# A hybrid backbone on one core: the first six filler steps of each layer take two PSUM banks in turn

## The chip, the cores and the metric

The kernel runs on one core of one Trainium2 chip. The metric is the device time of one execution in microseconds (us), as the median of several runs. Times inside an execution come from one profiled execution of the kernel before. PE is the matrix engine (TensorE), DVE the vector engine, ACT the scalar engine, POOL the GpSimd engine, SP the engine that issues most DMAs.

## The reference

Two layers of a diffusion backbone work on 1024 latent tokens of width 1024 and, in the first layer, on 256 context tokens too. Cut to what matters here:

```
def hybrid_layer(x, xc, ...):
    u  = modulate(rmsnorm(x,  n1), sh1, sc1)   @ w_in
    uc = modulate(rmsnorm(xc, n1), csh1, csc1) @ w_in
...
    ym, ymc = mlstm_mixer(...)      # 4 heads
    yn, ync = na_mixer(...)         # 8 heads, neighbourhood attention
    yl, ylc = lru_mixer(...)
    x = x + g1[:, None] * (jnp.concatenate([ym, yn, yl], axis=-1) @ w_out)
    x = x + g2[:, None] * sq_relu_mlp(modulate(rmsnorm(x, n2), sh2, sc2), w1, w2)
    if want_ctx:
        xc = xc + cg1[:, None] * (jnp.concatenate([ymc, ync, ylc], axis=-1) @ w_out)
        xc = xc + cg2[:, None] * sq_relu_mlp(modulate(rmsnorm(xc, n2), csh2, csc2), w1, w2)
```

The change concerns the product with `w_out`, and of it the part that needs only `ym` and `yl`: this half can be computed while the attention that makes `yn` is still running.

## The kernel before, in words

Activations lie feature by token. The token axis has blocks of 256 (context) and twice 512 (latent) columns, `BLKS`. A float32 product is made of three matmuls on split operands (a rounded high part and a low remainder): high times high, low times high, high times low. `load_w` loads a piece of weight (DMA, L197), ACT makes the high part (L200) and DVE the low part (L201). `split` does the same for activations (L210, L211).

PSUM has eight banks of 512 columns: one named p, one q, three a, two b, one c. `bank("pq")` takes the letters in turn, `bank("p")` always the same. Tiles of one bank are taken in the order of the program: a tile can be written when the one before it in the bank has been read.

Each layer has an attention stage, of four pairs of heads. `na_att` runs units of K x Q products (L825, L829, banks a), a softmax on DVE (L839, L843) and ACT (L846), transposes of the weights of attention (L718, `softmax_pv`, banks b, b, q in turn) and their product with V (L748, bank c). Between the units `side()` is called, 40 times in the first layer and 32 times in the second. It puts in a piece of `na_prep` for the next pair of heads and the steps of the filler that are due.

`na_prep` loads a piece of q or k (`ut`, DMA L672, two buffers), scales it on DVE (L675), transposes it on PE (L683, L685, bank b for the first pair of heads, then b, b, q in turn), splits it (L691, L692 for K, L696, L697 for Q), and copies parts to the other half of the partitions by DMA (L699, L702, L703). Positional bias tables (`tab`, L799) and V blocks (`VB`, L808) are loaded too.

The filler is `fill()`, which runs `oproj` on half 0 of the output projection. A step is twelve matmuls (L1354) into one tile of 256 or 512 columns, and then `ev_half`: a DMA load of the residual `xs` (L1370, three buffers, so the fourth load waits until the first store has gone), the eviction on DVE (L1371, scaled and added to `xs`), and the store (L1372). In the first layer the steps alternate between 256 and 512 columns for sixteen steps, and eight of 512 follow; in the second there are sixteen of 512. In the listings the first six steps of the first layer have the tiles 5946, 6107, 6208, 6365, 6520, 6599, those of the second 21757, 21936, 22100, 22248, 22436, 22615.

The order on each engine is not the order of the program. A scheduler places each instruction by its own estimates and keeps what data, buffers and banks demand. Each engine, and the queue of SP with its DMAs, then works its list strictly from the front: an instruction that waits holds all that stand behind it.

Of the kernel before, what the change touches and what calls it, by code (L numbers as in the profile page):

```python
# [91 lines left out]
def backbone_kernel(ctx: ExitStack, tc: tile.TileContext, I, out, dbg=None):  # L92
# [13 lines left out]
    def nm(s):  # L106
        seq[0] += 1
        return f"{s}_{seq[0]}"
# [17 lines left out]
    def bank(tag):  # L126

        if len(tag) > 1:
            turn[tag] = turn.get(tag, -1) + 1
            tag = tag[turn[tag] % len(tag)]  # L130
        return ps.tile([P, 512], F32, name=nm("ps" + tag), tag="ps" + tag, bufs=PSB[tag])
# [54 lines left out]
    def load_w(src, shape, early=False):  # L186


        raw = wp.tile([P, WSZ], F32, name=nm("wr"), tag="wr", bufs=2)
        hi = wp.tile([P, WSZ], F32R, name=nm("wh"), tag="wh", bufs=2)  # L190
        lo = wp.tile([P, WSZ], F32R, name=nm("wl"), tag="wl", bufs=2)
        n = shape[0] * shape[1]
        raw3 = raw[:, :n].rearrange("p (k c) -> p k c", k=shape[0])
        srcs = src if isinstance(src, list) else [src]
        m = shape[0] // len(srcs)
        for i, s_ in enumerate(srcs):
            sp.dma_start(raw3[:, i * m:(i + 1) * m], s_)  # L197
        cuts = [0, n // 4, n // 2, n] if early else [0, n]
        for a, b in zip(cuts, cuts[1:]):
            act.activation(hi[:, a:b], raw[:, a:b], AF.Copy)  # L200
            dve.tensor_sub(lo[:, a:b], raw[:, a:b], hi[:, a:b].bitcast(F32))  # L201
        return (hi[:, :n].rearrange("p (k c) -> p k c", k=shape[0]),
                lo[:, :n].rearrange("p (k c) -> p k c", k=shape[0]))
# [5 lines left out]
    def split(hi, lo, src32):  # L209
        act.activation(hi, src32, AF.Copy)  # L210
        dve.tensor_sub(lo, src32, hi.bitcast(F32))  # L211
# [236 lines left out]
    def wbank():  # L448
        wseq[0] += 1
        return bank("pqaaa")  # L450
# [155 lines left out]
    for l in range(DEPTH):  # L606
# [264 lines left out]
        with tc.tile_pool(name=f"m1_{l}", bufs=1, reuse_waits="tile") as m1:  # L871
            phase(f"lru_in{l}")

            with tc.tile_pool(name=f"lru_{l}", bufs=1, reuse_waits="tile") as lp, \
# [76 lines left out]
                for ct in range(2):  # L951
# [9 lines left out]
                    for d in range(2):  # L961
                        c4 = d * 2 + ct
                        gates = []
                        for gi in range(2):
# [3 lines left out]
                            for (o, n) in ((0, 512), (512, 512), (1024, 259)):  # L968
                                t = bank("a")
# [357 lines left out]
        def y_load(dst, blks, half, tp):  # L1327

            for i, (kt, r) in enumerate(YROWS[half]):
                if r == 7:  # L1330
                    continue
                for bi in blks:
# [2 lines left out]
                    sp.dma_start(yl_[:, :n], yT_d[l][r * P:(r + 1) * P, off:off + n])  # L1335
                    split(dst[bi][0][:, i], dst[bi][1][:, i], yl_[:, :n])

        def oproj(Y, blks, half, wide, evac, pre=None):

            for c2 in range(4):  # L1340
                cs = slice(c2 * 256, c2 * 256 + 256)
                rows = ((0, 2), (6, 8)) if half == 0 else ((2, 6),)
                w = load_w([I["w_out"][l, a * P:b * P, cs].rearrange("(k p) c -> p k c", p=P) for a, b in rows], (4, 256))
                if pre:
                    pre(blks, c2)
                for cc in range(2):
                    ct = c2 * 2 + cc
                    for bi in blks:
                        n = BLKS[bi][1]
                        t = wbank() if wide else bank("p")  # L1350
                        i = 0
                        for k in range(4):
                            for (a, b) in ((0, 0), (0, 1), (1, 0)):
                                pe.matmul(t[:, :n], w[a][:, k, cc * P:(cc + 1) * P], Y[bi][b][:, k],  # L1354
                                          start=(i == 0), stop=(i == 11))
                                i += 1
                        evac(t[:, :n], bi, ct)
                        yield
# [3 lines left out]
        with tc.tile_pool(name=f"na_{l}", bufs=1, reuse_waits="tile") as npl, \  # L1362
# [11 lines left out]
            def fill():  # L1374

                for part in parts:
                    phase(f"oproj{l}")
                    Yh = {bi: [yp.tile([P, 4, BLKS[bi][1]], F32R, name=nm("yh"), tag=f"yh{min(bi, 1)}{j}")
                               for j in range(2)] for bi in part}
                    y_load(Yh, part, 0, yp)  # L1380
                    for _ in oproj(Yh, part, 0, False, ev_half):
                        yield
                        phase(f"oproj{l}")
# [55 lines left out]
        with tc.tile_pool(name=f"mlp_{l}", bufs=1, reuse_waits="tile") as rp:  # L1439
# [12 lines left out]
            def oproj_end(blks, between=None):  # L1452
                def ev(t, bi, ct):
                    v = 1 if BLKS[bi][2] else 0
                    dve.scalar_tensor_tensor(xr[bi][:, ct], t, G1[:, ct, v:v + 1], xr[bi][:, ct],
                                             op0=OP.mult, op1=OP.add)
                    stat_add(acc2, bi, xr[bi][:, ct], ct, yk)

                for i, _ in enumerate(oproj(Y, blks, 1, True, ev, x_rows)):
                    if between and i == 2 * len(blks) - 1:  # L1460
                        between()
# [141 lines left out]
```

## Time and profile before

| what | us |
|---|---|
| median of 3 runs | 3117.27 |
| lowest and highest of the runs | 3112.53, 3120.43 |
| the profiled execution | 3115.3 |
| its span on the core | 3113.5 |
| PE busy in the span | 3013.0 |
| DVE busy | 1903.4 |
| ACT busy | 1130.1 |
| attention stage of layer 0, about | 505 to 745 |
| attention stage of layer 1, about | 2125 to 2345 |

The profiled execution lies 2.0 us below the median of the runs and 1.8 us above its own span. Busy time says how long an engine had an instruction running; a busy PE can run at either of two clock levels, and PEclk gives the mean granted clock as a share of the upper one.

### The profile page before, as it was taken

The numbers are of one execution on the slowest core, as the hardware profiler recorded it, in microseconds if no ns is written. First come the engines' busy times: TensorE is split into PE (matmuls) and PEld (weight loads), VectorE is DVE, ScalarE is ACT, GpSimd is POOL, SyncE is SP. The second block draws the span as 40 slices with busy tenths as digits, with TensorE's granted clock in tenths as the row PEclk, the third lists the DMA queues.
The fourth block names the chain that finished last, engine by engine and source line by source line (L and its number), as shares of the span: only waits on it lengthen the run. The fifth ranks groups of instructions, "written<-read, shape, count | busy, mean of one in ns | idle before, by whom it ended". The sixth has DMA issues, their size and how long they took to land.

```text
span 3113.5 us, 47480 instructions
## 1 busy us (share of the span) xinstructions
PE 3013.0 (97%) x18250; PEld 2550.8 (82%) x18250; DVE 1903.4 (61%) x4334; ACT 1130.1 (36%) x2027; POOL 283.9 (9%) x252
## 2 busy tenths in 40 slices
PE   7999998999999999999999999998899999999999
PEld 6888898877888888887778889997787777787777
DVE  6757654786977666555444484866788444444444
ACT  5632223565422222233233353234574222332222
POOL 0410010121200000010000411002222000000000
PEclk9999999999999999999999999999999999999999
DMA  8624567765233444233323542348763333333233
GB/s 273 216 73 134 175 187 204 217 179 185 68 109 109 122 129 122 78 112 95 95 88 96 161 143 81 98 129 231 220 179 99 95 95 93 97 115 93 90 96 93
DMA packets 506138, 410.72 MB, mean 132 GB/s; under 512 B 27197, under 2 KB 471577, under 8 KB 505913
## 3 DMA queue, kind: packets, MB, share of 16 engines
q1 hardware_dynamic: 494488, 387.41, 41.7%
q0 software_dynamic: 8576, 15.00, 1.5%
q10 hardware_dynamic: 2848, 5.28, 0.5%
q8 instruction: 144, 2.36, 0.3%
q14 instruction: 82, 0.66, 0.1%
HBM read 339.72 MB, written 67.53 MB: 131 GB/s over the span
## 4 chain that ended last, share of the span: by engine, by line
PE 71%; DVE 10%; DMA 9%; issue 2%; ACT 2%; SPq 1%; ACTq 0%; DVEq 0%
PE psa L461 15%; PE psa L1526 14%; PE psq L461 5%; PE psp L461 5%; PE psp L1526 5%; PE psq L1526 5%; PE psp L476 4%; PE psq L476 4%; DMA mr<-in_w_mod_dram 4%; PE psp L1354 2%; DVE ma L337 2%; PE psc L748 2%; PE psa L1354 1%; PE psb L718 1%; DVE wl L201 1%
## 5 line engine op out<-in xcount | busy, mean ns | idle before, releaser
L200 ACT ACTIVATE wh<-wr 128x1024 fp32r<-128x1024 f32 (+3 forms) x372 | 363.3, 985 | 927.1 <-PE psa L1526 311.3
L201 DVE TENSOR_TENSOR wl<-wr,wh 128x1024 fp32r<-128x1024 f32 (+3 forms) x372 | 426.8, 1152 | 386.2 <-ACT wh L200 379.7
L461 PE MATMUL psa<-xh,wh 128*128 128x512 f32 (+1 forms) x856 | 319.7, 374 | 2.4 <-ACT xh L436 2.2
L461 PE MATMUL psa<-xh,wl 128*128 128x512 f32 (+1 forms) x856 | 319.5, 374 | 1.4 <-DVE wl L201 1.4
L461 PE MATMUL psa<-xlo,wh 128*128 128x512 f32 (+1 forms) x856 | 320.0, 374 | 0.4 <-DVE xlo L437 0.4
L1526 PE MATMUL psa<-hl,wh 128*128 128x512 f32 (+1 forms) x768 | 286.2, 373 | 0.8 <-DVE hl L211 0.8
L1526 PE MATMUL psa<-hh,wh 128*128 128x512 f32 (+1 forms) x768 | 284.7, 376 | 0.3 <-ACT wh L200 0.3
L1526 PE MATMUL psa<-hh,wl 128*128 128x512 f32 (+1 forms) x768 | 278.1, 373 | 0.6 <-DVE wl L201 0.6
L1530 DVE SCALAR_TENSOR_TENSOR res<-psa,modt,res 128x512 f32<-128x512 f32 (+1 forms) x192 | 131.0, 693 | 170.1 <-PE psa L1526 169.9
L461 PEld LDWEIGHTS psa<-xh,wh 128*128 128x128 f32 x856 | 161.3, 188 | 34.1 <-ACT xh L436 2.4
L461 PEld LDWEIGHTS psa<-xh,wl 128*128 128x128 f32 x856 | 161.3, 189 | 33.0 <-DVE wl L201 2.2
L461 PEld LDWEIGHTS psa<-xlo,wh 128*128 128x128 f32 x856 | 161.5, 189 | 31.7 <-DVE xlo L437 0.6
L210 ACT ACTIVATE hh<-rl 128x512 fp32r<-128x512 f32 (+1 forms) x160 | 93.8, 589 | 220.4 <-DVE rl L1492 220.3
L1526 PEld LDWEIGHTS psa<-hh,wh 128*128 128x128 f32 x768 | 144.4, 188 | 34.7 <-ACT wh L200 8.7
L402 POOL TENSOR_TENSOR acc<-acc,nsq 128x512 f32<-128x512 f32 (+1 forms) x56 | 77.0, 1380 | 1024.5 <-ACT nsq L401 1023.8
L1526 PEld LDWEIGHTS psa<-hh,wl 128*128 128x128 f32 x768 | 144.5, 188 | 28.7 <-DVE wl L201 1.5
L1526 PEld LDWEIGHTS psa<-hl,wh 128*128 128x128 f32 x768 | 144.5, 188 | 27.6 <-DVE hl L211 1.1
L476 PE MATMUL psp<-wl,xh 128*128 128x256 f32 (+1 forms) x560 | 161.7, 289 | 5.4 <-DVE wl L201 5.2
L476 PE MATMUL psp<-wh,xh 128*128 128x256 f32 (+1 forms) x560 | 161.4, 288 | 3.3 <-ACT wh L200 3.3
L476 PE MATMUL psq<-wh,xh 128*128 128x256 f32 (+1 forms) x560 | 162.0, 289 | 1.2 <-ACT usq L632 0.7
L476 PE MATMUL psq<-wl,xh 128*128 128x256 f32 (+1 forms) x560 | 160.2, 286 | 0.0
L476 PE MATMUL psq<-wh,xlo 128*128 128x256 f32 (+1 forms) x560 | 159.9, 286 | 0.0
(409 smaller groups left out, 7326.1 us busy)
## 6 DMA issues: line engine op xcount, KB each, us to landing
wr<-in_w_mlp_dram SPq DMA_DIRECT2D x256, 512.0 KB
wr<-in_w_in_dram SPq DMA_DIRECT2D x48, 512.0 KB
mr<-in_w_mod_dram SPq DMA_DIRECT2D x48, 512.0 KB
mr<-in_w_mod_dram SPq DMA_DIRECT2D x22, 1024.0 KB
tab<-T_d SPq DMA_DIRECT2D x48, 384.0 KB
T_d<-E_d POOLq DMA_DIRECT2D x48, 256.0 KB, 6.6
ab<-row_d SPq DMA_DIRECT2D x36, 256.0 KB
xT_d<-res SPq DMA_DIRECT2D x4, 2048.0 KB
```

The lines of the kernel that those rows point to most:

```text
L200: act.activation(hi[:, a:b], raw[:, a:b], AF.Copy)
L201: dve.tensor_sub(lo[:, a:b], raw[:, a:b], hi[:, a:b].bitcast(F32))
L210: act.activation(hi, src32, AF.Copy)
L337: dve.scalar_tensor_tensor(a, raw[:, k], s[:, k], a, op0=OP.mult, op1=OP.add)
L402: pool.tensor_add(acc[bi], acc[bi], sq[:, :n])
L461: m = pe.matmul(t[:, :n], w[a][:, k, :], X[bi][b][:, k, :], start=(i == 0), stop=(i == 23))
L476: m = pe.matmul(t[:, :cols], X[bi][b][:, half * 4 + k, o:o + P], ws[half][a][:, k, :], start=(i == 0), stop=(i == 23))
L718: pe.transpose(t[:w, j * P:(j + 1) * P], S[e][:, o:o + w], permT)
L748: pe.matmul(to[64 * e:64 * e + 64, :P], vals[i][:w, 64 * e:64 * e + 64], PT[:w, e, i], start=(i == 0), stop=(i == nt - 1))
L1354: pe.matmul(t[:, :n], w[a][:, k, cc * P:(cc + 1) * P], Y[bi][b][:, k], start=(i == 0), stop=(i == 11))
L1526: m = pe.matmul(t[:, :n], w[a][:, k, cc * P:(cc + 1) * P], H[bi, k][b], start=(i == 0), stop=(i == 3 * GH - 1))
L1530: dve.scalar_tensor_tensor(xr[bi][:, ct], t[:, :n], G2[:, ct, v:v + 1], xr[bi][:, ct], op0=OP.mult, op1=OP.add)
```

## The change

A counter is put in for each layer, and the first six tiles that `oproj` takes outside the wide case come from `bank("pq")`. These are the first six filler steps of the layer: p, q, p, q, p, q. From the seventh on the bank is p, as before. Lines behind the edit move by four, so that the matmuls are L1358 and the eviction L1375.

```
+        n_half = [0]
+
         def oproj(Y, blks, half, wide, evac, pre=None):
...
                         n = BLKS[bi][1]
-                        t = wbank() if wide else bank("p")
+
+                        t = wbank() if wide else bank("pq" if n_half[0] < 6 else "p")
+                        n_half[0] += 1
                         i = 0
```

The number of instructions stays; their order in the two attention stages is new, and elsewhere it is as before. Three places show it.

DVE in layer 0, the difference of the two orders where the first `xs` load of those behind the K copies is used (L843 and L839 are attention's softmax):

```order
 L843 ISA S_6010,m_869_6012<-psa_5992,zcol,m_868_6011 128x256
 L843 ISA m_869_6012 128x1
-L1371 SCALAR_TENSOR_TENSOR xs_6378<-psp_6365,modt_119,xs_6378 128x512
+L1375 SCALAR_TENSOR_TENSOR xs_6533<-psp_6520,modt_119,xs_6533 128x256
 L839 ISA S_6088,m_886_6089<-psa_6074,tab_5984 128x384
 L839 ISA m_886_6089 128x1
```

The eviction of the fourth step (6365, 512 columns) is gone from here, and that of the fifth (6520, 256 columns) stands in its place; the second and fourth steps stand later, and the first, third and fifth have all gone by this point.

DVE in layer 1, at the first evictions, before (L692 and L697 make the low parts of K and Q, L675 scales a load):

```order
L1371 SCALAR_TENSOR_TENSOR xs_21770<-psp_21757,modt_120,xs_21770 128x512
L692 TENSOR_TENSOR KL_21515<-psb_21541,KH_21513 64x512
L697 SCALAR_TENSOR_TENSOR ql_21562<-psb_21557,gq_17233,QS_21511 64x512
L1371 SCALAR_TENSOR_TENSOR xs_21949<-psp_21936,modt_120,xs_21949 128x512
L697 SCALAR_TENSOR_TENSOR ql_21577<-psb_21572,gq_17233,QS_21510 64x512
L675 TENSOR_TENSOR ut_21648<-ut_21648,rsn_20574 128x256
L697 SCALAR_TENSOR_TENSOR ql_21577<-psb_21572,gq_17233,QS_21511 64x512
L675 TENSOR_TENSOR ut_21720<-ut_21720,rsn_20574 128x512
L1371 SCALAR_TENSOR_TENSOR xs_22113<-psp_22100,modt_120,xs_22113 128x512
```

The same place after:

```order
L1375 SCALAR_TENSOR_TENSOR xs_21770<-psp_21757,modt_120,xs_21770 128x512
L692 TENSOR_TENSOR KL_21515<-psb_21541,KH_21513 64x512
L697 SCALAR_TENSOR_TENSOR ql_21562<-psb_21557,gq_17233,QS_21511 64x512
L1375 SCALAR_TENSOR_TENSOR xs_22113<-psp_22100,modt_120,xs_22113 128x512
L697 SCALAR_TENSOR_TENSOR ql_21577<-psb_21572,gq_17233,QS_21510 64x512
L675 TENSOR_TENSOR ut_21648<-ut_21648,rsn_20574 128x256
L697 SCALAR_TENSOR_TENSOR ql_21577<-psb_21572,gq_17233,QS_21511 64x512
L675 TENSOR_TENSOR ut_21720<-ut_21720,rsn_20574 128x512
```

Before, the first three steps (21757, 21936, 22100) are evicted here; after, the first and the third are, and the second stands 81 rows behind the third.

SP in layer 1, with the K and Q copies of the pair of heads that follows (L699, L703) and the loads `ut_22345` and `ut_22417` of `na_prep`, before:

```order
L703 DMA KL_21647<-KL_21647 64x1280
L699 DMA QS_21643<-ql_21929 64x512
L672 DMA ut_22345<-u_nk_81 128x2x128
L1372 DMA xT_d<-xs_22628 128x512
L1370 DMA xs_22940<-xT_d 128x512
L197 DMA wr_23469<-in_w_out_dram 128x2x256 x2
L1370 DMA xs_23146<-xT_d 128x512
L197 DMA wr_23777<-in_w_out_dram 128x2x256 x2
L799 DMA tab_22304<-T_d_97 128x2x384
L672 DMA ut_22417<-u_nk_81 128x4x128
```

The same place after:

```order
L703 DMA KL_21647<-KL_21647 64x1280
L808 DMA VB_22157<-u_nv_83 32x4x128 x2
L672 DMA ut_22345<-u_nk_81 128x2x128
L699 DMA QS_21642<-ql_21929 64x512
L699 DMA QS_21643<-ql_21929 64x512
L672 DMA ut_22417<-u_nk_81 128x4x128
L699 DMA QS_21642<-ql_22024 64x512
L699 DMA QS_21643<-ql_22024 64x512
```

Before, four issues of `w_out` pieces (`wr`), two loads of `xs`, a store and a table stand between the two `ut` loads; after, the two stand close together, and the `w_out` pieces and `xs` loads come later.

## Rows read from the trace of the kernel before

**Rows 1.** The page: busy time by engine, and the chain's shares by engine

```profile
PE 3013.0 (97%) x18250; PEld 2550.8 (82%) x18250; DVE 1903.4 (61%) x4334; ACT 1130.1 (36%) x2027; POOL 283.9 (9%) x252
...
PE 71%; DVE 10%; DMA 9%; issue 2%; ACT 2%; SPq 1%; ACTq 0%; DVEq 0%
```

**Rows 2.** Line L1354: matmuls on p (ns), and idle before them, us, times

```profile
L1354 PE MATMUL psp<-yh,wh x320: 274/394/796, 514.8 to 2320.7; 128*128 128x512 f32 x128, 128*128 128x256 f32 x32
...
L1354 PE MATMUL psp<-yh,wl x160: 274/394/628, 516.0 to 2321.0; 128*128 128x512 f32 x128, 128*128 128x256 f32 x32
...
  DVE xs L1371: 17.5, 12
```

**Rows 3.** Stages: length, busy PE, PEld, DVE, ACT, POOL; PEclk, DMA share, GB/s

```profile
523.40:536.00 12.60, 8.98 (x65) 7.17 (x63) 8.68 (x18) 4.65 (x13) 6.96 (x4) 0.99 0.85 231
536.00:544.00 8.00, 5.35 (x23) 4.24 (x22) 3.49 (x15) 3.13 (x9) 0.00 (x0) 0.59 0.88 223
544.00:600.00 56.00, 55.33 (x452) 46.92 (x451) 44.78 (x137) 33.99 (x84) 11.02 (x6) 1.00 0.67 200
600.00:680.00 80.00, 71.43 (x591) 58.36 (x590) 68.98 (x216) 52.62 (x134) 14.53 (x8) 0.98 0.78 209
...
2150.00:2185.00 35.00, 33.76 (x262) 28.05 (x264) 29.82 (x88) 24.22 (x54) 5.07 (x2) 1.00 0.94 268
2185.00:2199.00 14.00, 9.68 (x43) 7.23 (x38) 12.31 (x31) 4.17 (x13) 3.61 (x2) 0.63 0.72 207
2199.00:2260.00 61.00, 56.99 (x463) 47.12 (x463) 47.97 (x143) 36.53 (x90) 14.62 (x8) 1.00 0.73 214
```

**Rows 4.** The chain in order of time, layer 0: start, duration, what

```profile
519.10 4.41 PE psp L1354 x12
...
569.04 1.43 PE psp L1354 x12
...
602.67 8.13 DMA KL<-KL
...
716.76 2.78 PE psp L1354 x12
```

**Rows 5.** SP in order of time, layer 0: start, duration, what, times

```profile
539.77 1.41 SPq L1370 DMA_DIRECT2D xs<-xT_d  x3
```

**Rows 6.** DVE in order of time, layer 0, with idle before and releaser

```profile
542.59 0.75 DVE L1371 SCALAR_TENSOR_TENSOR xs<-psp,modt,xs 128x512 f32<-128x512 f32 x1 [4.09 <-DMA xs<-xT_d]
```

**Rows 7.** PE in order of time, layer 1

```profile
2175.76 0.37 PE L829 MATMUL psa<-KH,QS 128*128 128x256 f32 x1
...
2188.38 0.69 PE L825 MATMUL psa<-KH,QS 128*128 128x384 f32 x1 [2.44 <-DVE m L839]
...
2191.42 0.58 PE L829 MATMUL psa<-KH,QS 128*128 128x256 f32 x1 [1.40 <-DVE m L843]
```

**Rows 8.** DVE in order of time, layer 1

```profile
2170.43 0.75 DVE L1371 SCALAR_TENSOR_TENSOR xs<-psp,modt,xs 128x512 f32<-128x512 f32 x1
...
2171.99 1.22 DVE L201 TENSOR_TENSOR wl<-wr,wh 128x1024 fp32r<-128x1024 f32 x1
...
2176.97 0.43 DVE L675 TENSOR_TENSOR ut<-ut,rsn 128x256 f32<-128x256 f32 x1 [2.16 <-DMA ut<-u_nk]
...
2186.14 1.68 DVE L675 TENSOR_TENSOR ut<-ut,rsn 128x512 f32<-128x512 f32 x1 [3.63 <-DMA ut<-u_nk]
```

**Rows 9.** Waits of PE, layer 1: us in total, times, longest

```profile
PE psa L825 <- DVE m L839: 5.0, 3, 2.4
```

**Rows 10.** SP in order of time, layer 1

```profile
2178.02 0.89 SPq L197 DMA_DIRECT2D wr<-in_w_out_dram  x2
...
2179.50 0.46 SPq L672 DMA_DIRECT2D ut<-u_nk  x1
```

**Rows 11.** The MLP of layer 0, columns as in rows 3

```profile
1100.00:1150.00 50.00, 50.00 (x287) 43.40 (x287) 34.13 (x82) 13.83 (x22) 0.00 (x0) 1.00 0.43 125
```

**Rows 12.** One group of PE in these 50 us: busy, mean ns | idle before

```profile
L461 PE MATMUL psp<-xh,wh 128*128 128x256 f32 (+1 forms) x16 | 5.4, 336 | 0.0
```

## The prediction

> **What bounds the kernel now.** I read the page first: TensorE is busy for 3013.0 us of a span of 3113.5, and the chain that ended last lies on PE for 71% and on DVE for 10% [rows 1]. So a change can win only idle PE time or time at the lower clock, about 100 us in all, and can lose by adding to either. Next I read the line that the change touches: L1354 has 320 + 160 matmuls on bank p, and before them PE stood idle 17.5 us, in 12 places, until an eviction (L1371) had emptied the bank [rows 2]. That is the wait which the second bank can remove. It is 0.6% of the span, and not all of it can be had, since only six steps of each layer are touched.
>
> Third, the busy time by stage over the two stretches where these steps stand [rows 3]. In layer 0, PE works 8.98 of 12.60 us up to 536, 5.35 of 8.00 at a mean granted clock of 0.59 up to 544, then 55.33 of 56, and again only 71.43 of 80 up to 680. In layer 1 it works 33.76 of 35 us up to 2185, then 9.68 of 14 at 0.63, then 56.99 of 61. The idle stretches are those in which attention waits for data, and the filler steps are what PE does meanwhile. Whether a step runs inside such a hole or after it decides what it costs.
>
> The price of a step is read from the chain in order of time [rows 4]: twelve matmuls of 512 columns take 2.78 us at the upper level (2.4 GHz), twelve of 256 columns 1.43, and the step at 519.10, after PE had idled, took 4.41, mostly at the lower level (1.2 GHz).
>
> **The change, layer 0.** No instruction is added; every second of six tiles goes to bank q. But q is also the bank of the next heads' transposes and of every third softmax tile, tiles of one bank are taken in program order, and the order is written anew. What comes out shows in the order of DVE. The landmark there is the eviction that uses the first xs load that SP issues behind the K copies, three at 539.77 [rows 5]: DVE stood 4.09 us for it, until 542.59, with attention's softmax queued behind it [rows 6]. That load keeps its place behind the same copies. In the old order it serves the fourth step's eviction, so PE has by then done four steps (256, 512, 256, 512 columns); in the new one it serves the fifth's, and the second and fourth, on q, come later: three steps of 256. The old order owed PE nothing at that point; the new one owes 2 x 2.8 less the 256-step done early, 1.4: 4.2 us of matmuls. They come in 544 to 600, where only 0.67 us is idle, so they sit on the path.
>
> Against this, DVE has one 0.75 us eviction fewer ahead of the landmark and the loads of one preparation are issued a little earlier: I take the landmark as 1.0 us earlier, bounds 0 and 4.1 (DVE's whole wait for it; below zero is excluded, since nothing is put ahead of the copies). With fewer matmuls to do while attention waits, new idle of 0.5 us, bounds 0 and 3. Sum: 4.2 - 1.0 + 0.5 = **+3.7 us**. The best end also regains the 0.7 idle and the 2.2 us that PE loses to the lower level in 536 to 544 (5.35 x 0.41): 4.2 - 4.1 - 0.7 - 2.2 = -2.8. The worst end is three steps in the open, 3 x 2.8 = +8.4.
>
> **The change, layer 1.** All steps have 512 columns. In the order, the second step's eviction has left its place and the third step's stands there instead; the second, fourth and sixth steps wait for bank q, and the steps behind them wait with them, because the three xs buffers go round: the fifth step's is the second's. By the K x Q product at 2175.76 [rows 7] the old order has done seven steps, the new one two: five steps, 5 x 2.8 = 14.0 us, are owed. In exchange DVE passes this stretch without three evictions of 0.75 and three weight splits of 1.22 [rows 8], 5.9 us together, and attention gets that far earlier; since DVE was not full there (29.82 of 35, [rows 3]) I take 4 of the 5.9, bounds 0 and 5.9.
>
> Then comes the hole. Before, PE waited 2.44 and 1.40 us for the softmax [rows 7], because DVE stood 2.16 and 3.63 us until preparation loads (ut) had landed [rows 8]; over the layer's stage the K x Q products wait 5.0 us for it, in three places [rows 9]. SP issues the second one at 2179.50, behind w_out loads [rows 10], and it lands at 2186.14 [rows 8], 6.6 us later. In the new order both ut loads stand ahead of those w_out loads. So part of the hole closes, and what is left of it is filled with owed steps. From 2175.8 to 2260 are 84.2 us. They hold 4.3 idle (2185 to 2199), 4.0 idle (2199 to 2260), and 4.2 lost to the clock: 0.63 over 14 us means 10.4 us at the lower level, some 8.4 of it busy, and half of that is loss. Work: 84.2 - 8.3 - 4.2 = 71.7, plus 14.0 owed is 85.7 us. Residual idle I take as 3 us (between 0, all holes filled, and 12.5, all of idle and clock loss still there). The stretch then ends at 2175.8 - 4 + 85.7 + 3 = 2260.5, **+0.5 us**; bounds 2175.8 - 5.9 + 85.7 = 2255.6 (-4.4) and 2175.8 + 85.7 + 12.5 = 2274.0 (+14.0).
>
> **Sum.** +3.7 + 0.5 = +4.2 us, bounds -7.2 and +22.4. Against the profiled execution, 3115.3 us, that is 3119.5. The median of the runs, 3117.3, lies 2.0 above it, and the same sum there gives 3121.5; I take 3120, between the two. The other edits of the diff (a counter and a choice of bank) cost the chip nothing.
>
> **Rivals.** *A, holes close fully.* The ut loads come early enough for DVE never to wait, so layer 1 goes to its best end, -4.4, and in layer 0 the owed 4.2 us fall into the 8.6 idle us of 600 to 680, where the chain goes through transfers (a K copy of 8.13 us, [rows 4]) and not through PE; with the landmark 4.1 earlier and the clock's 2.2 regained that is -6.3. Together -10.7: 3117.3 - 10.7 = 3106.6. For it: the early ut loads. Against it: 544 to 600 is full and lies before that hole, and PE then moves everything behind it.
>
> *B, the cover is gone.* Slower: the filler is what kept PE at work while attention waited for transfers. If attention stays bound by its loads and DVE (the DMA share is 0.94 in 2150 to 2185, [rows 3]), PE idles where the five steps stood, the clock falls sooner, and the steps come when PE is full. Layer 1 then costs its upper end, +14.0, layer 0 its 3.7: +17.7, 3135. The place is 2139 to 2176; it decides from about 8 us of residual idle instead of 3. For it: in the new order PE has no other work there. Against it: DVE's 5.9 us.
>
> *C, the clock falls because banks alternate.* Layer 0's MLP ran 50.00 of 50 us at a granted clock of 1.00 [rows 11] while it wrote p, q and a in turn (by `wbank`; its share on p is in [rows 12]), so alternation alone does not lower it here. Were it so, nine 512-steps would cost 4.41 - 2.78 = 1.63 more each and three 256-steps half that, together 17.1: 3137. The Trainium skill, "TensorE: Matmul & The Clock Gate", section "A second HAM failure mode: psum-queue depth-cycling", tells of a kernel that cycled through PSUM banks and idled so often between groups that its clock swung between the two levels. By that rule this would be the outcome; the stage at 1.00 does not bear it out.
>
> *D, nothing that counts.* The steps change places inside the same stage, and gains and debts cancel within 2 us: 3117.
>
> **Chances.** Forecast and D together 0.66 (0.45 and 0.21), A 0.14, B 0.17, C 0.03. About 0.3%, 9.4 us, is what a measurement of this kernel can tell from no change: below 3107.9 counts as faster, above 3126.6 as slower. Faster is A, 0.14; slower is B and C, 0.20; within is 0.66. The range from 3107 to 3132 takes in the bounds of the sum but for its far upper part, where B and C lie (some 0.12 is above it, 0.06 below).
>
> **What would show it.** Right: PE's idle until the L1371 eviction (L1375 in the new file) falls well under 17.5 us; three 256-steps precede the xs landmark; 536 to 544 has less PE work, 544 to 600 stays full; in layer 1 the waits of 2.16 and 3.63 on ut are gone or short and the stretch 2185 to 2199 has no stall of 2.44. Wrong: PE idle beyond 3 us between 2176 and 2260, or over 8 us more in 2139 to 2176 without attention coming earlier (B); a mean clock under 0.9 in 544 to 600 (C); or both stages ending early (A).

## The result: slower by 0.7%

The changed kernel takes 3139.7 us against 3120.0 for the kernel before (medians of six runs each): +19.7 us, a ratio of 1.0072 with an interval of 1.0056 to 1.0087. The forecast was 3120 with a range up to 3132. The profiled execution took 3139.4 us, its span is 3137.6, 24.1 above the span before; the profiled execution of the kernel before lies 4.7 us below its median, so the two profiles differ by 4.4 us more than the medians do.

The first rows are from the page of the kernel after: busy time by engine, and the shares of the chain that ended last.

```profile
PE 3022.3 (96%) x18250; PEld 2561.4 (82%) x18250; DVE 1901.3 (61%) x4334; ACT 1132.4 (36%) x2027; POOL 283.0 (9%) x252
...
PE 72%; DVE 10%; DMA 9%; issue 2%; ACT 2%; SPq 1%; ACTq 0%; DVEq 0%
```

The same 18250 matmuls keep PE busy 9.3 us longer than in [rows 1], at a mean granted clock of 0.985 in place of 0.991, so some ran at the lower clock level that had not; the rest of the 24.1 us is idle time. The view of the line of the output projection, with the idle time before it that the evictions ended:

```profile
L1358 PE MATMUL psp<-yh,wh x272: 274/394/628, 517.0 to 2346.1; 128*128 128x512 f32 x104, 128*128 128x256 f32 x32
...
L1358 PE MATMUL psq<-yh,wh x48: 390/394/502, 554.8 to 2242.6; 128*128 128x512 f32 x48
...
  DVE xs L1375: 16.2, 16
```

Six steps (48 matmuls with the high weights) went to q, the first of them at 554.8, where the second step of the kernel before began at 519.1 [rows 4]. And the wait for evictions hardly fell: 16.2 us where it was 17.5 [rows 2]. Both figures add up the idle time of PE and that of its weight loads (PEld), which run side by side. The views of PE's own waits give, before, in layer 0 and in layer 1 (us in total, times, longest):

```profile
PE psp L1354 <- DVE xs L1371: 3.5, 4, 1.6
PE psp L1354 <- DVE xs L1371: 4.3, 2, 2.8
```

The same after:

```profile
PE psp L1358 <- DVE xs L1375: 3.7, 4, 2.2
PE psp L1358 <- DVE xs L1375: 4.6, 4, 2.4
```

So PE itself stood 7.8 us for evictions in the kernel before, not 17.5, and stands 8.3 us now.

Where the time went is read from busy time by stage. From the first filler step to the end of its stage layer 0 takes 236.3 us in place of 224.1, and layer 1 209.0 in place of 197.5: +12.2 and +11.5, nearly all of the 24.1. I cut each stage in two, in layer 0 at the eviction for which DVE waits (542.6 before, 545.0 after), in layer 1 at the K x Q product that stood at 2175.0 and now stands at 2187.3. The columns are those of rows 3; the rows of layer 1 stop some 6 us ahead of the end of its stage, in both kernels. The kernel before:

```profile
514.80:542.60 27.80, 21.00 (x104) 16.68 (x104) 17.66 (x42) 11.65 (x30) 7.29 (x4) 0.75 0.88 235
542.60:738.90 196.30, 186.26 (x1542) 156.41 (x1543) 158.90 (x519) 124.43 (x321) 36.56 (x20) 0.99 0.65 185
2126.20:2175.00 48.80, 40.56 (x248) 32.26 (x248) 38.34 (x90) 24.43 (x53) 21.71 (x12) 0.97 1.01 264
2175.00:2317.60 142.60, 132.45 (x1131) 110.90 (x1131) 118.02 (x387) 90.99 (x238) 32.70 (x18) 0.96 0.68 195
```

The kernel after:

```profile
517.00:545.00 28.00, 16.81 (x90) 13.72 (x90) 16.56 (x41) 11.27 (x29) 7.23 (x4) 0.70 0.99 247
545.00:753.30 208.30, 194.07 (x1557) 163.87 (x1558) 156.99 (x520) 124.87 (x322) 36.34 (x20) 0.97 0.61 173
2140.00:2187.30 47.30, 32.57 (x178) 25.06 (x179) 30.44 (x79) 19.84 (x45) 20.18 (x11) 0.75 0.85 217
2187.30:2342.90 155.60, 146.40 (x1201) 121.67 (x1200) 127.29 (x400) 97.29 (x246) 33.34 (x18) 0.99 0.69 196
```

The first half of each stage is about as long as before (+0.2 and -1.5 us), with much less PE work in it (21.0 to 16.8 and 40.6 to 32.6 us busy) and a lower clock (0.75 to 0.70, 0.97 to 0.75). The second half is longer by 12.0 and 13.0 us, and there PE is busy for longer: the work that was missing early has come back.

Single instructions, PE in order of time. The start of step two of layer 1 in the kernel before:

```profile
2132.89 0.99 PE L1354 MATMUL psp<-yh,wh 128*128 128x512 f32 x2 [2.82 <-DVE xs L1371]
```

The kernel after:

```profile
554.83 0.71 PE L1358 MATMUL psq<-yh,wh 128*128 128x512 f32 x2
...
626.61 0.43 PE L825 MATMUL psa<-KH,QS 128*128 128x352 f32 x1 [3.64 <-DVE m L839]
...
2162.09 0.66 PE L825 MATMUL psa<-KH,QS 128*128 128x384 f32 x1 [2.99 <-DMA QS<-ql]
...
2168.01 0.69 PE L825 MATMUL psa<-KH,QS 128*128 128x384 f32 x1 [3.76 <-DVE m L839]
...
2189.48 0.63 PE L1358 MATMUL psq<-yh,wh 128*128 128x512 f32 x2
```

and DVE:

```profile
544.98 0.48 DVE L1375 SCALAR_TENSOR_TENSOR xs<-psp,modt,xs 128x256 f32<-128x256 f32 x1 [4.34 <-DMA xs<-xT_d]
...
625.39 0.69 DVE L675 TENSOR_TENSOR ut<-ut,rsn 128x512 f32<-128x512 f32 x1 [5.65 <-DMA ut<-u_nq]
...
2166.82 0.69 DVE L675 TENSOR_TENSOR ut<-ut,rsn 128x512 f32<-128x512 f32 x1 [4.89 <-DMA ut<-u_nk]
```

Step two of layer 1 began at 2132.9 before and begins at 2189.48 now. Ahead of it PE stands for data of attention, 2.99 and 3.76 us, with no step to run.

### The profile page after: what moved, and what is told of

It reads as the page before. It is cut to its first block, busy times and chain, and to the rows that moved or that the text cites. A ratio compares the mean times of both kernels' runs of the same rounds, so it can differ in the third digit from the quotient of the medians.

```text
span 3137.6 us, 47477 instructions
## 1 busy us (share of the span) xinstructions
PE 3022.3 (96%) x18250; PEld 2561.4 (82%) x18250; DVE 1901.3 (61%) x4334; ACT 1132.4 (36%) x2027; POOL 283.0 (9%) x252
## 4 chain that ended last, share of the span: by engine, by line
PE 72%; DVE 10%; DMA 9%; issue 2%; ACT 2%; SPq 1%; ACTq 0%; DVEq 0%
PE psa L461 15%; PE psa L1530 14%; PE psq L461 5%; PE psp L461 5%; PE psp L1530 5%; PE psq L1530 5%; PE psp L476 4%; PE psq L476 4%; DMA mr<-in_w_mod_dram 4%; PE psp L1358 2%; DVE ma L337 2%; PE psc L748 2%; PE psa L1358 1%; DMA ut<-u_nq 1%; PE psb L718 1%
## 5 line engine op out<-in xcount | busy, mean ns | idle before, releaser
L1530 PEld LDWEIGHTS psa<-hl,wh 128*128 128x128 f32 x768 | 144.4, 188 | 27.8 <-DVE hl L211 0.9
```

The lines of the kernel that those rows point to most:

```text
L1530: m = pe.matmul(t[:, :n], w[a][:, k, cc * P:(cc + 1) * P], H[bi, k][b], start=(i == 0), stop=(i == 3 * GH - 1))
```

## The experiments

Medians below are from runs beside the kernel before (3119.2 to 3122.0 us); a ratio is to that kernel, with its interval.

**One layer at a time.** `e1_layer0` and `e2_layer1`:

```
-  bank("pq" if n_half[0] < 6 else "p")
+  bank("pq" if l == 0 and n_half[0] < 6 else "p")     # e2: l == 1
```

> The two banks in turn for the first six steps of layer 0 alone; layer 1 as before. Theory (held steps: the second, fourth and sixth step wait in bank q behind the transposes of the next pair of heads, PE idles where they stood and does them later, when it is full): the trace after put +11.9 us of the change into layer 0's attention stage, so 3120 + 12 = 3132, and layer 1's stage as long as before (190.8 us from the first filler step to the end of the stage, against 202.3 after). Rival (the slowdown is spread or comes from one layer alone, the other only shifts): 3120 or 3140.

> The two banks in turn in layer 1 alone. Theory (held steps): +11 us, 3131, layer 0 as before. Rival (one layer alone costs): 3120 or 3140. Together with the run on layer 0 the two should add up to the +20 to +24 of both layers if each stage is by itself.

Measured 3133.5 (1.0042, 1.0025 to 1.0059) and 3131.6 (1.0032, 1.0019 to 1.0045), against 3121.5: +12.0 and +10.0. The two add up to the whole, so each layer pays for itself, and whatever explains it must hold in both. The stages with the change took 242.9 us (layer 0 of e1) and 214.2 (layer 1 of e2), those without it 203.1 (layer 1 of e1) and 222.8 (layer 0 of e2); the first two profiles had 236.3 and 209.0 with it, 197.5 and 224.1 without. A single stage thus varies by up to some 7 us from one execution to the next, so smaller differences between stages of two profiles say nothing by themselves.

**Late steps without a second bank.** `e9_held_p` is the kernel before, with one scheduling tie more:

```
-  if len(anchors) > 30:
+  if len(anchors) > 30 or 2 <= n_half[0] < 3:
       with tc.issue_after(anchors[-1 - 0]):
           next(filler, None)
```

> Bank p alone, as in the kernel before, but the third filler step of each layer is tied behind the attention unit at which the program issues it, and with one bank the later steps follow it. In the order the steps then stand about where the change put them (layer 1: two before the first unit's products, the third after six units; the change: two, then the next two after six units). Theory (what costs is that the steps come late, not the second bank): most of the change's +20 returns, 3132 to 3145. Rival (the second bank itself costs): 3120, as before.

Measured 3138.9 against 3122.0 (1.0061, 1.0041 to 1.0082): +16.9 us, with bank p alone. What the two kernels have in common is seen in the time that PE spends on the filler's line in the first 60 us of each stage. The columns are length, PE busy (matmuls), weight loads, clock, DMA share, GB/s; layer 0, then layer 1. The kernel before:

```profile
514.80:574.80 60.00, 25.66 (x117) 19.90 (x118) 0.89 0.79 223
2126.20:2186.20 60.00, 26.72 (x96) 18.43 (x96) 0.97 0.99 266
```

The kernel after:

```profile
517.00:577.00 60.00, 19.59 (x84) 15.82 (x84) 0.83 0.79 211
2140.00:2200.00 60.00, 15.75 (x48) 10.54 (x48) 0.80 0.82 206
```

e9:

```profile
518.00:578.00 60.00, 17.06 (x72) 13.03 (x72) 0.83 0.73 192
2143.70:2203.70 60.00, 13.12 (x44) 8.55 (x44) 0.83 0.87 228
```

With the second bank 84 + 48 matmuls run there in place of 117 + 96, with one bank and the tie 72 + 44; PE has 17.0 us less of this work in the one and 22.2 in the other, and the clock falls alike. Holding the steps back by a tie is enough for most of the slowdown; no second bank is needed. But the tie rewrites the order too: DVE stands 21.2 and 26.0 us for preparation loads (ut) in the two stages of e9, where it stood 10.0 and 19.4 before and stands 22.7 and 20.2 in the kernel after. So e9 alone does not tell the late steps from the new places of these waits.

**Only two steps alternate.** `e5_two` has `n_half[0] < 2`.

> Only the first two steps of each layer alternate, so one step per layer goes to bank q in place of three. In the order that step is held, but the steps on p overtake it, since their bank and their xs buffers are free: four steps stand by the second unit of layer 0, as before. Theory (held steps cost by the work that is missing early): nothing is missing, 3118 to 3124. Rival (each step on q costs by itself): a third of +20, 3127.

Measured 3133.1 against 3122.0 (1.0033, 1.0014 to 1.0052): +11, more than either theory. In the first 60 us only 9 and 15 matmuls are missing (108 and 81), and layer 0's stage is as long as before (225.8), but layer 1's is 218.9 us (a stretch that holds 34 matmuls more than the 1425 of the kernel before), and the profile shows more waits there for preparation loads than the kernel before had (DVE stood 30.5 us for ut in place of 19.4). My theory does not foresee this; it is the first sign that the order written anew costs by itself.

**Bank q for the filler alone.** `e3_noq_p` (control) and `e4_noq_pq`:

```
-  t = bank("b" if hp < 1 else "bbq")     # na_prep
+  t = bank("b")
...
-  t = bank("bbq")                        # softmax_pv
+  t = bank("b")
```

> Control for the next run: the preparation's transposes and the softmax tiles no longer use bank q (bank b alone, two buffers), and the filler stays on p. Bank q lies idle in attention. Both theories: the order of the first filler steps stays as before; attention has two banks in place of three for its transposes, so somewhat slower, 3120 to 3135.

> As the run before, and the first six steps write p and q in turn, with q now the filler's alone. Theory (held steps): no step is held, four steps stand before the first preparation in layer 1 where the control has two, so not slower than the control: 0 to -6 us against it. Rival (taking two banks in turn is itself the cost, by evictions that collide on DVE or by the clock): +20 us against the control, as the change cost.

Measured 3174.7 (1.0165, 1.0144 to 1.0186) and 3183.0 (1.0200, 1.0181 to 1.0220). Taking q from attention costs 53 us, far more than I expected; of the waits of PE in layer 1 of e3 (us, times, longest) the largest is the filler's for its evictions on bank p, and the next are those of the transposes and the products with V for DVE's copies:

```profile
PE psp L1354 <- DVE xs L1371: 10.8, 3, 3.9
PE psb L718 <- DVE PT L737: 5.8, 4, 2.7
PE psc L748 <- DVE PT L737: 5.6, 4, 2.6
```

So the kernel needs q where it was, in attention. Between the two the second bank costs 8 us, where I had expected a gain and the rival 20. It tells little, since attention sets the pace in both; but it speaks against a gain from a free second bank.

**The steps ahead of the preparation.** `e11_front_p` (control, bank p) and `e10_front_pq`, which put the first six steps into the program before the first `na_prep` piece:

```
+  while hp == 0 and n_half[0] < 6:
+      next(filler, None)
   phase(f"na_prep{l}")
...
-  for _ in range(due("fill")):
+  for _ in range(due("fill") if (pace["at"] + 1) * pace["fill"] // n_side > n_half[0] else 0):
```

> The first six steps stand in the program ahead of the first piece of preparation, all at the first unit, and alternate p and q. Bank q is still shared, but now the steps are ahead of the transposes in its order. Theory (steps are held because they stand behind the transposes in q's order): nothing is held, so against the same placing on p alone (next run) -5 to +5 us. Rival (alternation itself costs): +20 against it.

> Control for the run before: six steps ahead of the first preparation, all on p. Theory: the evictions still pace the steps on one bank, so little changes against the kernel before, 3115 to 3130; the steps are spent somewhat earlier and can be missed later.

Measured 3117.5 on p (0.9987, 0.9973 to 1.0002: not told from the kernel before) and 3129.5 on both banks (1.0029, 1.0014 to 1.0044): +12 us by the second bank, where I expected none. The steps are early here, 94 and 72 matmuls in 30 us against 72 and 64 of the control, so lateness is not the reason. Now attention is behind. The 17th matmul of line L825 (K x Q) in layer 1 starts 51.1 us after the first step against 41.2 of the control. All PE work in these stretches, control and then e10:

```profile
2127.10:2168.30 41.20, 32.59 (x187) 25.87 (x187) 27.84 (x62) 16.26 (x33) 20.28 (x12) 0.96 0.97 273
```

```profile
2137.30:2188.40 51.10, 41.89 (x191) 32.37 (x189) 31.88 (x64) 17.83 (x34) 20.52 (x12) 0.83 0.92 256
```

Of the 9.9 us, 9.3 are busy time of PE: in e10 eight filler steps are done ahead of that product, in the control six, and the mean clock is 0.83 in place of 0.96. The longest wait of PE in this stretch of e10 is for the high part of the steps' own weights:

```profile
2158.81 1.22 PE L1358 MATMUL psp<-yh,wh 128*128 128x512 f32 x2 [4.08 <-ACT wh L200]
```

Such waits come to 6.5 us in layer 1 of e10 and to 1.1 in the control. So here the steps, no longer paced by each other's eviction, ran ahead of their weights, with attention queued behind them. Whether attention's transposes, held in bank q, add to the cost, as steps are held in the change, is not shown.

**A third buffer for the preparation loads.** `e13_ut3_p`, `e14_ut3_pq` and `e15_ut3_front_p` (the last on e11) have `tag="ut", bufs=3` in place of 2.

> A third buffer for the preparation loads (ut), so that a load is issued a piece earlier and DVE stands less for it; filler on p. DVE stood for these loads 10.0 us in layer 0 and 19.4 in layer 1 of the kernel before. Control for the next run: 3105 to 3122.

> The change with a third ut buffer; the first steps are held as in the change (layer 1: two by the first unit, four after six units). Theory 1 (held steps: PE has nothing to do early, and the debt is paid when it is full): against the control still +15 to +22. Theory 2 (the cost comes in where DVE's waits for ut fall in the new order: in layer 0 these waits grew from 10.0 to 22.7 us): the buffer takes most of it away, +0 to +10 against the control, layer 0's part going first.

> Third ut buffer, and six filler steps ahead of the first preparation, on p alone. Theory 1: early cover is worth having and DVE's waits for ut are shorter, 3100 to 3117, faster than the kernel before. If neither counts: 3120.

Measured 3136.0 (1.0045, 1.0030 to 1.0059), 3149.4 (1.0089, 1.0069 to 1.0109) and 3121.3 (1.0001, 0.9986 to 1.0016). The buffer doesn't do what it was meant for: in layer 1 of e13 DVE still stands longer for these loads than before (19.4).

```profile
DVE ut L675 <- DMA ut<-u_nk: 21.9, 7, 7.0
...
DVE ut L675 <- DMA ut<-u_nq: 3.0, 2, 2.8
```

So the pair doesn't test that cause. The second bank again costs 13 us on top of it. The control itself says something else: e13 has no second bank and no step held (118 and 91 matmuls of the filler in the first 60 us, before 117 and 96), and costs 16 us. A new order, here one that follows from a buffer more, can cost almost as much as the change.

**The waits for loads at fixed places.** `e16_soft_p` (control) and `e17_soft_pq` tie every scaling of a preparation load behind the softmax of the unit that issues it, so that these waits stand at the same places of DVE's list in both:

```
-  dve.tensor_mul(uv, uv, rsn[kd, grp]...)
+  with (tc.issue_after(softs[-1]) if softs else nullcontext()):
+      dve.tensor_mul(uv, uv, rsn[kd, grp]...)
...
-  dve.tensor_tensor_reduce(out=s_[:, nl:nl + 256], ...)
+  sm_ = dve.tensor_tensor_reduce(out=s_[:, nl:nl + 256], ...)
+  softs.append(sm_.ins)
```

> Every scaling of a preparation load (ut, DVE) is tied behind the softmax of the attention unit at which the program issues it, so that DVE's waits for these loads stand at the same places of its list whatever the filler does. Filler on p; its steps stand as in the kernel before (four by the second unit of layer 0, and in layer 1 four by the third). Control for the next run; the preparation comes evenly and later: 3105 to 3130.

> The same with the first six steps on p and q in turn. DVE's list of ut scalings and softmax steps is the same as in the control but for one place; the steps are held as in the change (layer 1: two by the first unit, four after six units). Theory 1 (held steps alone cost): layer 0 about +8 by the steps missing after 60 us (2.8 steps), layer 1 about +11 (4 steps), together +15 to +22 against the control. Theory 2 (the places of DVE's ut waits in the new order cost most): 0 to +8.

Measured 3119.8 (1.0006, 0.9991 to 1.0021) and 3128.3 (1.0022, 1.0011 to 1.0034): +8.5 us by the second bank, between the two theories. DVE's waits for ut in layer 0 are nearly gone in both (they were 10.0 us in the kernel before and 22.7 in the one after). e16, and then e17:

```profile
DVE ut L677 <- DMA ut<-u_nq: 1.7, 1, 1.7
DVE ut L677 <- DMA ut<-u_nk: 1.0, 1, 1.0
```

```profile
DVE ut L677 <- DMA ut<-u_nk: 3.8, 2, 2.2
DVE ut L677 <- DMA ut<-u_nq: 0.2, 1, 0.2
```

And yet layer 0's stage grows by 11.6 us between them. All work in it, e16 and e17:

```profile
520.40:743.80 223.40, 202.81 (x1648) 172.24 (x1648) 173.48 (x560) 136.69 (x351) 43.65 (x24) 0.96 0.71 192
```

```profile
518.10:753.10 235.00, 212.19 (x1646) 177.29 (x1647) 178.15 (x560) 136.07 (x351) 45.38 (x24) 0.93 0.67 183
```

PE is busy 9.4 us longer there for the same 1648 matmuls, at a mean clock of 0.93 in place of 0.96. So in layer 0 waits for ut are not needed for a loss of this size. In layer 1 the two stages are alike (205.9 and 204.4), though 48 matmuls of the filler stand in the first 60 us against 96. That does not show that the owed work found holes, since the control's stage is itself 8.4 us longer than that of the kernel before (197.5).

## Why the prediction was wrong

**What bounds the kernel** held. The bound is PE, a gain could only be idle or slow-clock time, and the loss came in as these.

**The wait to be removed was read too large.** The 17.5 us in 12 places of [rows 2] are 7.8 us of PE and 9.7 of its weight loads, in six places each. PE's own 7.8 us are 0.25% of the span, not 0.6%. The sum did not use the figure, but the reason for a gain rested on it, and the wait did not fall: 8.3 us after.

**The order was read rightly.** The steps on q stand behind the transposes in their bank, and three steps of 256 columns precede the landmark of layer 0. The debts have the forecast size: PE is busy 21.0 - 16.8 = 4.2 us less up to the landmark, as worked out (at mean clocks of 0.75 and 0.70, so the exact match is partly luck). In the first half of layer 1 the filler has done 24 matmuls in place of 84, the five steps of the forecast; PE is busy only 8.0 us less there, not 14.0, since it worked more at the lower level (0.75 after 0.97).

**Layer 0, the landmark:** taken as 1.0 us earlier, it is 0.2 us later in the stage (28.0 against 27.8). DVE stands 4.34 us for the load, where it was 4.09 [rows 6].

**Layer 0, behind the landmark: a step that failed.** I took this part as the old one plus the owed 4.2 us and 0.5 of new idle (at most 3); it grew by 12.0. PE is busy 7.8 us longer, which is the 4.2 and 3.6 more at the lower level (clock 0.99 to 0.97), and idle 14.2 us in place of 10.0: 4.2 of new idle. The sum has no term for the lower level, nor for anything behind 600 us, as if the order were the old one again there. It was not. The largest waits of PE behind the landmark, of which the kernel before has the first not at all and the second with 1.0 us:

```profile
PE psc L748 <- DMA VC<-u_nv: 5.2, 2, 4.0
PE psa L825 <- DVE m L839: 3.6, 1, 3.6
```

The first is for loads of the context's V blocks; no run tested it. For the second, the scaling of one preparation load had moved ahead of two softmax reductions, DVE stood 5.65 us for it (625.39), and PE 3.64 behind that (626.61). e16 and e17 show that this wait is not needed for a loss: nearly without waits for ut, layer 0 still paid 11.6 us by the second bank. The whole layer's +12.2 lies beyond the worst end of its sum, +8.4.

**Layer 1: the terms that failed are the lead and what I let the hole give back.** The owed 14.0 us came out whole: behind the cut PE is busy 146.4 us against 132.5, 13.9 more. Against it I had set a lead of 4 us and a hole that closes but for 3 of 12.5 us. The lead is 1.5 us (47.3 against 48.8), because PE, with no steps to run, waited for copies and loads of attention, and worked at the lower level when they came: up to the cut it was idle 14.7 us in place of 8.2. DVE was relieved as forecast, by more than the 5.9 us (38.3 to 30.4 us busy up to the cut), and attention still came only 1.5 us earlier. The long waits of the hole did go. The largest waits of PE behind the cut, kernel before:

```profile
PE psa L829 <- DVE m L843: 3.3, 2, 1.9
PE psa L825 <- DVE m L839: 2.9, 2, 2.4
```

The same, kernel after:

```profile
PE psp L1358 <- DVE xs L1375: 2.2, 3, 0.9
PE psb L718 <- DVE PT L737: 1.9, 2, 1.4
PE psq L718 <- DVE KL L692: 1.3, 1, 1.3
```

But other, shorter ones took their place, and the idle time fell only from 10.2 to 9.2 us. I booked a hole as gained because the wait at its end would vanish; the next wait was right behind it.

**Rival B was the nearest,** at +17.7 us against +19.7 measured: the filler is cover for attention's waits, and when it is late PE idles first and is overfull later. e9 shows this with one bank, though not free of the new order. That the number fits is partly luck: B had 14.0 us in layer 1 and 3.7 in layer 0, where the profile has 11.5 and 12.2. What B did not have is that the second bank also costs with the steps early (e10, +12) or with few of them late (e5, +11). A and D are ruled out by the time. In all five pairs of a kernel with and without the second bank for the six steps it costs 8 to 20 us.

**Rival C** (the clock falls because banks alternate) is not borne out: the steps on q run at the upper level. One of them in the chain in order of time of the kernel after:

```profile
555.08 2.80 PE psq L1358 x12
```

2.80 us for twelve matmuls, as 2.78 on p [rows 4]. The mean clock is low (0.70 and 0.75) in the first halves of the stages, where PE idles and no step on q stands, and 0.97 and 0.99 in the second halves, where all six do. The Trainium skill, "TensorE: Matmul & The Clock Gate", section "A second HAM failure mode: psum-queue depth-cycling", tells of a kernel that cycled through banks and idled so often between groups that its clock swung; the trace agrees that the low clock goes with idle stretches, and does not show that taking banks in turn lowers it where PE stays at work.

**What stays open.** How much of the +19.7 us is the held work and how much the order that falls out of it: no run holds the steps and leaves the rest of the order as it was, and e13 paid 16 us for an order without held work. With DVE's waits at fixed places the second bank cost 8.5 us, without that 12 to 20; layer 1 paid in the change and not in e17, beside a control that was slow there. Why two steps alone cost 11 us (e5) is not shown. That one bank is better because each step must wait for the eviction of the last, which spreads the steps over attention's holes, fits e4, e10 and the change, but no run measured it by itself.

## What to carry to other kernels

A filler is worth what it covers: before giving it another buffer, read how long the engine itself waits for the buffer (not the sum with its weight loads), ask which work holds that buffer in program order, and list how many steps stand ahead of each wait in the old and the new order, since a step that moves behind a hole is paid at full length later. Count work that is owed at its price, but don't count the hole that it may fall into until the next wait behind that hole has been named. And where a scheduler writes the order, a small edit rewrites it far from its place, so compare the whole stage, not the part up to where the names seem to match again.

## What was not expected of the hardware

Without its third transpose bank attention makes the kernel 53 us longer (e3), where I had expected at most 15. And taking DVE's waits for preparation loads away bought nothing: they are 10.0 and 19.4 us in the two layers before and 2.7 and 1.9 in e16, and the time stays the same, 3119.8 against 3119.2. The ties that took them away let other waits of DVE grow (for the filler's matmuls from 9.7 to 21.5 us), so this does not show what the waits for loads cost by themselves.
